# DeepNorm hybrid layer on one core: the seven-product scheme of the FFN output projection, in two groups of eight blocks with its left sums stored in DRAM

## The chip, the cores and the metric

The kernel runs on one core of a Trainium2 chip (trn2). The metric is the device time of one execution in microseconds (us); the kernel before was timed in three runs. TensorE does the matrix products (PE in the profile; its weight loads are PEld), VectorE is DVE, ScalarE is ACT, GpSimd is POOL, and SyncE is SP, whose queue issues nearly every DMA of this kernel.

## What is computed

One encoder layer on a sequence of 1024 positions and a model width of 1024: an FFN half step, attention beside a state-space scan with an output projection, a second FFN half step and a gated embedding, each followed by a layer norm. The change touches the two FFN half steps alone:

```python
def _swiglu(x, w_in, w_out):
    gate, up = jnp.split(x @ w_in, 2, axis=-1)
    return (jax.nn.silu(gate) * up) @ w_out
...
x = _layer_norm(ALPHA * x + 0.5 * _swiglu(x, ffn1_w_in[i], ffn1_w_out[i]), ln_g[i, 0], ln_b[i, 0])
...
x = _layer_norm(ALPHA * x + 0.5 * _swiglu(x, ffn2_w_in[i], ffn2_w_out[i]), ln_g[i, 2], ln_b[i, 2])
```

The hidden width is 2816, which is 22 blocks of 128. Below, h is silu(gate) * up, kept transposed: block f holds 128 hidden units by 1024 positions.

## The kernel before

**Split operands.** Every product is of float32 precision. An operand is split into a rounded part (a copy to fp32r on ACT, L100 or L400) and a remainder (a subtraction on VectorE, L82 or L401), and `mm3` (L108 to L115) issues three matmuls for each pair of blocks: high by low, low by high, high by high. A matmul of 128x128 by 128x512 is the unit of TensorE's work here.

**Making h** (`ffn_h`, `ffn_first`, `ffn_rest`). Each block f takes seven products of 12 matmuls (a seven-product scheme over the two column halves of w_in and the two halves of the positions). The weights of f come by two DMAs of 512 KB from SP (`raw`, L92); GpSimd makes their sums (L246 to L249) and adds two of the products (L331, L332); VectorE empties PSUM (L271, L326, L330, L333, L334) and multiplies (L336, L337); SP stores block f to `hD` in DRAM (L338, one DMA of 512 KB). The split weights stand in a ring of 10 buffers (`blk`), the products in four PSUM buffers (`sm`). Meanwhile, two iterations for each step, `right_sums` loads two blocks of w_out (L293, L294), makes four sums of their halves on VectorE (L299 to L302) and stores them in `wT` (L287).

**The product h by w_out** (`ffn_strassen`, then a tail). The first 16 blocks of h go through a seven-product scheme once more, in four groups of four blocks. In a group, two blocks of h make the first column of a 2 by 2 matrix of halves and two the second, and likewise with w_out. Each of the seven products has 24 matmuls (four column chunks of 128, two blocks, three passes). Three of them (called "11", "12" and "21" after the part of the result) are added from the PSUM tiles `sm` to the accumulators `acc` (L415, four 512-wide additions on VectorE); the other four go from the PSUM tiles `big`, of which there are two, to sums called M1, M5, M6 and M7: in the first group by ACT (L419), then by VectorE (L421, two 1024-wide additions). A product's left operand is a half of h as it is or a sum of halves; the sums are made here by GpSimd (`combine`, L451), which also makes some of the remainders (L401). The operands live in eight tiles named xh00 to xl11 (`pair`), two to a product, so operands for four products can be there at once. After the last group the M are added to each other (`add_sums`, L427) and to the accumulators (`add`, L432). The other six blocks of h go through the tail: two blocks in 16 units of 6 matmuls (first tail; `ffn_out`, L364 empties PSUM), then four blocks, with the layer norm.

**What sets the order.** TensorE's order is that of the code (`in_order`). The other engines' queues are laid out by a scheduler when the program is built; each engine then works through its queue in order. `issue_after` (`behind`) holds a DMA behind the SP instruction traced last. SP has one queue, so a DMA that waits for its source holds up all behind it.

Of the kernel before, what the change touches and what calls it, by code (L numbers as in the profile page):

```python
# [25 lines left out]
GRP = 2  # L26
# [10 lines left out]
class Layer:  # L37
# [236 lines left out]
    def right_sums(self, c, i, wo, groups):  # L274
# [5 lines left out]
        to = self.dram.tile([groups, 4, P, 2, 512], F32, name=f"wT{i}")  # L280
# [9 lines left out]
        def load(q):  # L290
            g, j = divmod(q, 2)
            w1, w2 = (pool.tile([P, D], F32, name=n) for n in ("wr1", "wr2"))
            nc.sync.dma_start(out=w1, in_=wo[4 * g + j])  # L293
            nc.sync.dma_start(out=w2, in_=wo[4 * g + 2 + j])  # L294
            return w1, w2, pool.tile([P, 2, 512], F32, name="wt12")

        def sums(q, w1, w2, t):
            g, j = divmod(q, 2)
# [9 lines left out]
        def step(n):  # L308
            q = n // 2
            if n % 2:  # L310
                return sums(q, *tiles[q])
            with self.behind(mybir.EngineType.SP):
                store()
                if q < 2 * groups:
                    tiles[q] = load(q)

        return pool, to, [lambda n=n: step(n) for n in range(4 * groups + 1)]

    def ffn_rest(self, X, tmp, to, blocks, p1, sg, between=None):
# [18 lines left out]
        nc.sync.dma_start(out=to, in_=sg)  # L338

    def ffn_h(self, X, wi, tmp, hD, pre=(), done=0, aside=None):  # L340
# [8 lines left out]
        for f in range(done, NF + 1):  # L349
            s = first(f) if f < NF else None  # L350
            self.pop(2)
            if prev:
                self.ffn_rest(X, tmp, hD[f - 1], self.mixed_blocks(*prev[0]), *prev[1:])
# [12 lines left out]

# [11 lines left out]
    def ffn_strassen(self, c, hD, wo, wT, acc, groups, tp, during):  # L380
# [3 lines left out]
        V, G, A = nc.vector, nc.gpsimd, nc.scalar  # L384
# [6 lines left out]
        C = {"11": (0, lo), "12": (0, hi), "21": (4, lo), "22": (4, hi)}  # L391

        def split(srcs, n, eng):

            b = self.pair()
            for i, src in enumerate(srcs):
                o = slice(0, n) if len(srcs) < n or n == 1 else slice(i, i + 1)
                if len(src.shape) == 2:
                    src = src.unsqueeze(1)
                A.copy(out=b[:, o, 0], in_=src)  # L400
                eng.tensor_tensor(out=b[:, o, 1], in0=src, in1=b[:, o, 0].bitcast(F32), op=ALU.subtract)  # L401
            return b

        def product(S, T, n, to, first=False):

            for jp in range(2):
                ps = None if to in C else self.psb()
                for q in range(2):
                    o = self.pss() if to in C else ps[:, q * 512:(q + 1) * 512]
                    c = slice((jp * 2 + q) * P, (jp * 2 + q + 1) * P)  # L410
                    self.mm3(o, [((S[:, b, 0, c], S[:, b, 1, c]), (T[:, b, 0], T[:, b, 1])) for b in range(n)])
# [22 lines left out]
        def right(g, k):  # L434
            t = tp.tile([P, 2, 512], F32, name="wT", bufs=3)
            nc.sync.dma_start(out=t, in_=wT[g, k])
            return t

        for gi, fs in enumerate(groups):
            n = len(fs) // 2  # L440
            first = fs is groups[0]
            h1 = [self.ring_raw(hD[f]) for f in fs[:n]]
            w1 = self.ring.tile([P, 2, 512], F32, name="blk")
            for i, f in enumerate(fs[:n]):
                nc.sync.dma_start(out=w1[:, i], in_=wo[f][:, lo])
            h2, w2 = [self.ring_raw(hD[f]) for f in fs[n:]], [self.ring_raw(wo[f]) for f in fs[n:]]
            s1, s2 = (tp.tile([P, 2, 512], F32, name=k)[:, :n] for k in ("s1", "s2"))

            def combine(out, a, b, op=ALU.subtract, eng=G):
                for i in range(n):  # L450
                    eng.tensor_tensor(out=out[:, i], in0=a(i), in1=b(i), op=op)  # L451

            a11, a21 = (lambda i: h1[i][:, lo]), (lambda i: h1[i][:, hi])
            a12, a22 = (lambda i: h2[i][:, lo]), (lambda i: h2[i][:, hi])
            b21, b22 = (lambda i: w2[i][:, lo]), (lambda i: w2[i][:, hi])

            def raw(x, eng=V):
                return split([x(i) for i in range(n)], n, eng)

            E = V if first else G  # L460
            last = fs is groups[-1]
            t2, t4, t1 = right(gi, 1), right(gi, 3), right(gi, 0)
            product(raw(a11), split([w1], n, V), n, 1, first)
            combine(s1, a21, a22, ALU.add)
            combine(s2, lambda i: s1[:, i], a11)
            product(raw(a12), raw(b21), n, "11")
            product(split([s2], n, V), split([t2], n, V), n, 6, first)
            t3 = right(gi, 2)
            combine(s2, a12, lambda i: s2[:, i])
            product(raw(a22, E), split([t4], n, V), n, "21")  # L470
            product(split([s1], n, V), split([t1], n, V), n, 5, first)
            combine(s1, a11, a21)
            product(split([s2], n, V), raw(b22, G), n, "12")
            if last:
                add_sums(6, 1)
                add_sums(5, 6)
            product(split([s1], n, V), split([t3], n, V), n, 7, first)
# [4 lines left out]
    def ffn_y(self, c, i, x, hD, wo, wT, weights, groups, after=None):  # L482
# [6 lines left out]
        for t in range(NT):  # L489
# [1213 lines left out]
```

## Time and profile before

| | |
|---|---|
| median of 3 runs | 2087.12 us (2084.81 to 2087.18) |
| the profiled execution, its own time | 2087.78 us |
| its span, first to last instruction | 2085.9 us |
| mean granted TensorE clock | 0.991 |
| h of FFN 1 made, until | about 476 us |
| seven-product stage of FFN 1 | 476.0 to 632.2 us |
| its first tail | 632.2 to 660.4 us |
| seven-product stage of FFN 2 | 1752.0 to 1908.7 us |
| its first tail | 1908.7 to 1936.9 us |

A row of the view by stretches gives, for a stretch of the span, its length, each engine's busy time with its number of instructions in brackets, TensorE's granted clock, the DMA engines' share and their rate. In the list of waits a row names who waited, the line and engine that ended the wait, the total, the number of waits and the longest. A matmul's shown duration (0.39 us) overlaps the next one's, so the pace of TensorE is read from how many stand in a stretch.

### The profile page before, as it was taken

The numbers are of one execution on the slowest core, as the hardware profiler recorded it, in microseconds if no ns is written. First come the engines' busy times: TensorE is split into PE (matmuls) and PEld (weight loads), VectorE is DVE, ScalarE is ACT, GpSimd is POOL, SyncE is SP. The second block draws the span as 40 slices with busy tenths as digits, with TensorE's granted clock in tenths as the row PEclk, the third lists the DMA queues.
The fourth block names the chain that finished last, engine by engine and source line by source line (L and its number), as shares of the span: only waits on it lengthen the run. The fifth ranks groups of instructions, "written<-read, shape, count | busy, mean of one in ns | idle before, by whom it ended". The sixth has DMA issues, their size and how long they took to land.

```text
span 2085.9 us, 25640 instructions
## 1 busy us (share of the span) xinstructions
PE 2014.4 (97%) x9312; PEld 1643.4 (79%) x9316; DVE 1561.8 (75%) x2353; ACT 874.8 (42%) x1610; POOL 619.7 (30%) x440
## 2 busy tenths in 40 slices
PE   7899999999999999998999999899999999999998
PEld 6688888888787888787887777778888888877886
DVE  6865565658899838648997769886666666989987
ACT  5433333336441214528888864333333334533121
POOL 0544444426530213000001001264444444541111
PEclk9999999999999999999999999999999999999999
DMA  7323433447531311230003381133334329542222
GB/s 256 118 101 122 160 123 121 151 153 282 190 122 58 119 42 36 76 96 33 1 1 104 105 302 72 71 111 141 121 121 162 121 91 341 194 141 81 71 81 81
DMA packets 94822, 254.33 MB, mean 122 GB/s; under 512 B 11586, under 2 KB 24258, under 8 KB 94696
## 3 DMA queue, kind: packets, MB, share of 16 engines
q1 hardware_dynamic: 92392, 248.51, 33.8%
q10 hardware_dynamic: 2304, 4.20, 0.5%
q8 instruction: 73, 1.20, 0.2%
q14 instruction: 53, 0.43, 0.1%
HBM read 184.84 MB, written 67.83 MB: 121 GB/s over the span
## 4 chain that ended last, share of the span: by engine, by line
PE 79%; DVE 11%; ACT 4%; DMA 3%; issue 2%; POOL 1%; SPq 0%; DVEq 0%; ACTq 0%; POOLq 0%
PE sm L114 59%; PE big L114 9%; PE big L1024 3%; PE sm L1046 3%; DVE blk L82 2%; PE sm L1061 1%; PE sm L1062 1%; DVE M L427 1%; DVE acc L415 1%; POOL qr L753 1%; DVE M L421 1%; DVE xl L82 1%; PE big L202 1%; DMA sg<-in_wi_dram 1%; ACT y L1124 1%
## 5 line engine op out<-in xcount | busy, mean ns | idle before, releaser
L114 PE MATMUL sm<-xh,blk 128*128 128x512 f32 x1440 | 452.7, 395 | 0.0
L114 PEld LDWEIGHTS sm<-xh,blk 128*128 128x128 f32 x1440 | 271.6, 189 | 64.3
L114 PE MATMUL sm<-xl,blk 128*128 128x512 f32 x720 | 285.6, 397 | 2.6 <-DVE xl L82 2.6
L114 PE MATMUL sm<-blk,xh 128*128 128x512 f32 (+2 forms) x912 | 279.1, 383 | 5.1 <-DVE blk L82 4.7
L114 PE MATMUL sm<-xl,xh 128*128 128x512 f32 x960 | 232.7, 393 | 8.0 <-DVE acc L364 7.2
L100 ACT CAST blk<-raw 128x512 fp32r<-128x512 f32 (+1 forms) x168 | 100.6, 611 | 327.9 <-PE sm L114 181.9
L114 PEld LDWEIGHTS sm<-xl,xh 128*128 128x128 f32 x960 | 178.4, 188 | 51.3 <-DVE acc L364 14.9
L114 PEld LDWEIGHTS sm<-blk,xh 128*128 128x128 f32 x912 | 169.3, 191 | 39.2 <-DVE blk L82 6.5
L82 DVE TENSOR_TENSOR blk<-s,blk 128x512 fp32r<-128x512 f32 x176 | 147.4, 841 | 69.0 <-ACT blk L100 67.2
L82 DVE TENSOR_TENSOR blk<-raw,blk 128x512 fp32r<-128x512 f32 (+1 forms) x168 | 148.6, 895 | 57.6 <-ACT blk L100 56.9
L114 PE MATMUL big<-xl,xh 128*128 128x512 f32 x768 | 180.5, 392 | 6.3 <-DVE M L421 5.2
L100 ACT CAST blk<-s 128x512 fp32r<-128x512 f32 x176 | 108.4, 622 | 161.1 <-PE sm L114 148.5
L114 PEld LDWEIGHTS big<-xl,xh 128*128 128x128 f32 x768 | 145.0, 189 | 37.7 <-ACT xl L400 6.0
L114 PE MATMUL sm<-blk,xl 128*128 128x512 f32 (+2 forms) x456 | 172.8, 379 | 0.0
L114 PEld LDWEIGHTS sm<-xl,blk 128*128 128x128 f32 x720 | 135.8, 189 | 36.2 <-DVE xl L82 4.2
L246 POOL TENSOR_TENSOR s<-raw 128x512 f32<-128x512 f32 x42 | 56.2, 1338 | 289.5 <-DVE blk L82 204.6
L177 POOL TENSOR_TENSOR ln_k<-ln_k,mhalf 128x1 f32<-128x1 f32 x32 | 40.5, 1264 | 317.3 <-DVE ln_k L176 296.7
L114 PE MATMUL sm<-xET3h,blk 128*128 128x512 f32 x352 | 110.7, 395 | 0.2 <-DVE blk L82 0.2
L114 PE MATMUL sm<-xET2h,blk 128*128 128x512 f32 x352 | 110.5, 395 | 0.1
L114 PEld LDWEIGHTS sm<-blk,xl 128*128 128x128 f32 x456 | 87.0, 191 | 15.3
L249 POOL TENSOR_TENSOR s<-raw,s 128x512 f32<-128x512 f32 x42 | 58.9, 1402 | 132.3 <-DVE blk L82 132.1
L331 POOL TENSOR_TENSOR u<-u,p 128x512 f32<-128x512 f32 x44 | 73.8, 1677 | 79.8 <-DVE u L330 79.8
(310 smaller groups left out, 4063.5 us busy)
## 6 DMA issues: line engine op xcount, KB each, us to landing
raw<-in_wi_dram SPq DMA_DIRECT2D x84, 512.0 KB
hD<-sg SPq DMA_DIRECT2D x44, 512.0 KB
blk<-hD SPq DMA_DIRECT2D x44, 512.0 KB
wr<-in_wo_dram SPq DMA_DIRECT2D x32, 512.0 KB
wT<-wT SPq DMA_DIRECT2D x32, 512.0 KB
blk<-in_wo_dram SPq DMA_DIRECT2D x28, 512.0 KB
wT<-wt SPq DMA_DIRECT2D x32, 256.0 KB
wT<-wr SPq DMA_DIRECT2D x32, 256.0 KB
```

The costliest lines, as they stand in the source:

```text
L82: (eng or self.nc.vector).tensor_tensor(out=out, in0=full, in1=hi.bitcast(F32), op=ALU.subtract)
L100: self.nc.scalar.copy(out=b[:, 0, :n], in_=src)
L114: self.nc.tensor.matmul(ps, lhsT=a, rhs=b, start=(i == 0), stop=(i == n - 1))
L177: nc.gpsimd.tensor_tensor(out=r, in0=v, in1=self.mhalf[:, :1], op=ALU.pow)
L202: nc.tensor.transpose(out=ps[:, k], in_=a[:, k * P:(k + 1) * P], identity=self.ident)
L246: G.tensor_tensor(out=s1, in0=a21, in1=a22, op=ALU.add)
L249: G.tensor_tensor(out=s4, in0=a12, in1=s2, op=ALU.subtract)
L331: G.tensor_tensor(out=u2, in0=u2, in1=p5, op=ALU.add)
L415: V.scalar_tensor_tensor(out=a, in0=o, scalar=scale, in1=a, op0=ALU.mult, op1=ALU.add)
L421: V.scalar_tensor_tensor(out=m, in0=ps, scalar=scale, in1=m, op0=ALU.mult, op1=ALU.add)
L1024: nc.tensor.matmul(ps[:, n * 512:(n + 1) * 512], lhsT=Q[:, h, q0:q0 + P], rhs=K[:, h // 4, j, n * 512:(n + 1) * 512], start=j == 0, stop=j ...
L1046: nc.tensor.transpose(out=pt[:, k], in_=pr[:, kk * P:(kk + 1) * P], identity=self.ident)
```

## The change

**Groups.** The 16 blocks go in two groups of eight instead of four groups of four. The even blocks of a group are the first column of the 2 by 2 matrix, the odd ones the second, so the sums of h take neighbouring blocks. A product has 48 matmuls, and its operands take four of the eight tiles xh00 to xl11. The number of matmuls and the sizes of the tiles are as before; each sum M and each accumulator is added to half as often.

**Left factors.** `left_factors` makes the sums of h in `ffn_h`, on VectorE, as soon as a block is there: one for an even block, three for an odd one (tiles h1, h2, h3). All seven left factors of a group go to `hS` in DRAM: two DMAs of 256 KB for an even block and five for an odd one, where one DMA of 512 KB stood before. Blocks 16 to 21 go to `hD` as before. The pool of h tiles (`sg`) has three buffers in both FFNs (before: two in the first, three in the second).

**Streaming.** Each product loads its own operands (`operand`): two DMAs of 512 KB for the left, two of 512 KB or four of 256 KB for the right, into ring tiles; then ACT copies and VectorE subtracts, four times each, 1024 wide. GpSimd has no work in this stage. The accumulators' initial values are loaded in quarters (`load`), each just ahead of the product that adds to it first, where they were all loaded ahead of the stage.

The diff, cut to its core:

```diff
-    def right_sums(self, c, i, wo, groups):
+    def right_sums(self, c, i, wo):
...
-            nc.sync.dma_start(out=w1, in_=wo[4 * g + j])
-            nc.sync.dma_start(out=w2, in_=wo[4 * g + 2 + j])
+            nc.sync.dma_start(out=w1, in_=wo[2 * q])
+            nc.sync.dma_start(out=w2, in_=wo[2 * q + 1])
...
+    def left_factors(self, i, tmp):
...
+        def store(f, h):
+            if f >= NS:
+                nc.sync.dma_start(out=hD[f - NS], in_=h)
+                return
+            g, j = divmod(f // 2, GRP // 2)
+
+            def put(k, src):
+                nc.sync.dma_start(out=hS[g, k, :, j], in_=src)
+
+            def combine(name, a, b, op=ALU.subtract):
+                t = tmp.tile([P, 512], F32, name=name)
+                V.tensor_tensor(out=t, in0=a, in1=b, op=op)
+                return t
+
+            if f % 2 == 0:
+                put(0, h[:, lo])
+                put(6, combine("h3", h[:, lo], h[:, hi]))
+                even.append(h)
+            else:
+                e = even.pop()
+                put(1, h[:, lo])
+                put(3, h[:, hi])
+                s1 = combine("h1", e[:, hi], h[:, hi], ALU.add)
+                s2 = combine("h2", s1, e[:, lo])
+                put(4, s1)
+                put(2, s2)
+                put(5, combine("h3", h[:, lo], s2))
...
-        nc.sync.dma_start(out=to, in_=sg)
+        to(sg)
...
+        def operand(src):
+
+            blocks = []
+            for u in range(n // 2):
+                r = self.ring.tile([P, 2, 512], F32, name="blk")
+                src(u, r)
+                b = self.pair()
+                A.copy(out=b[:, :, 0], in_=r)
+                V.tensor_tensor(out=b[:, :, 1], in0=r, in1=b[:, :, 0].bitcast(F32), op=ALU.subtract)
+                blocks += [b[:, i] for i in range(2)]
+            return blocks
...
+            L, R = operand(left), operand(right)
...
-                    self.mm3(o, [((S[:, b, 0, c], S[:, b, 1, c]), (T[:, b, 0], T[:, b, 1])) for b in range(n)])
+                    self.mm3(o, [((l[:, 0, c], l[:, 1, c]), (r[:, 0], r[:, 1])) for l, r in zip(L, R)])
...
-            combine(s1, a21, a22, ALU.add)
-            combine(s2, lambda i: s1[:, i], a11)
-            product(raw(a12), raw(b21), n, "11")
-            product(split([s2], n, V), split([t2], n, V), n, 6, first)
...
+        for g in range(NS // GRP):
+            first, last = g == 0, g == NS // GRP - 1
+            f = g * GRP
+            for k, right, to in ((0, plain(f, lo), 1), (1, plain(f + 1, lo), "11"), (2, summed(wT[g, 1]), 6), (3, summed(wT[g, 3]), "21"),
+                                 (4, summed(wT[g, 0]), 5), (5, plain(f + 1, hi), "12"), (6, summed(wT[g, 2]), 7)):
+                if first and to in C:
+                    with self.behind(mybir.EngineType.SP):
+                        load(*C[to])
+                if last and k == 6:
+                    add_sums(6, 1)
+                    add_sums(5, 6)
+                product(summed(hS[g, k]), right, to, first)
...
-        out = c.enter_context(tc.tile_pool(name=f"fo{i}", bufs=n))
+        out = c.enter_context(tc.tile_pool(name=f"fo{i}", bufs=3))
```

**The order at three places.** First, the place where one group gives way to the next, in FFN 1. Before, VectorE's queue from the end of the second group's "12" to the start of the third group (M70 and M71 are the two halves of M7, the group's last product, M10 and M11 those of M1, the next group's first; `big` are the PSUM tiles they come from; xh00 to xl01 are operands of later products):

```order
L415 SCALAR_TENSOR_TENSOR acc0_2_3653<-sm_4234,acc0_2_3653 128x512
L415 SCALAR_TENSOR_TENSOR acc0_3_3654<-sm_4242,acc0_3_3654 128x512
L401 TENSOR_TENSOR xh00_4397<-s2_4308,xh00_4397 128x2x512
L401 TENSOR_TENSOR xl00_4400<-wT_4309,xl00_4400 128x2x512
L421 SCALAR_TENSOR_TENSOR M70_3673<-big_4264,M70_3673 128x1024
L421 SCALAR_TENSOR_TENSOR M71_3674<-big_4278,M71_3674 128x1024
L401 TENSOR_TENSOR xl01_4448<-wT_4311,xl01_4448 128x2x512
L421 SCALAR_TENSOR_TENSOR M10_3683<-big_4323,M10_3683 128x1024
```

Now there is one such place in a stage, behind the first group, where M7 is taken from PSUM by ACT. ACT's queue there (L469 is what L419 was, L439 the copy of a split; xh10 to xl11 are operands of the second group's first product, xh00 to xl01 of the one after it):

```order
L439 CAST xl10_4344<-blk_4342 128x2x512
L439 CAST xl11_4356<-blk_4353 128x2x512
L469 ACTIVATE M70_3774<-big_4273 128x1024
L439 CAST xh00_4413<-blk_4411 128x2x512
L439 CAST xh01_4424<-blk_4421 128x2x512
L469 ACTIVATE M71_3775<-big_4299 128x1024
L439 CAST xl00_4418<-blk_4416 128x2x512
L439 CAST xl01_4430<-blk_4427 128x2x512
```

and VectorE's, up to the second addition to M1 (L440 is the subtraction of a split, L471 the addition to a sum M; the L83 rows split a weight of the stage that follows):

```order
L440 TENSOR_TENSOR xl11_4356<-blk_4353,xl11_4356 128x2x512
L440 TENSOR_TENSOR xh00_4413<-blk_4411,xh00_4413 128x2x512
L440 TENSOR_TENSOR xh01_4424<-blk_4421,xh01_4424 128x2x512
L440 TENSOR_TENSOR xl00_4418<-blk_4416,xl00_4418 128x2x512
L440 TENSOR_TENSOR xl01_4430<-blk_4427,xl01_4430 128x2x512
L471 SCALAR_TENSOR_TENSOR M10_3784<-big_4359,M10_3784 128x1024
L83 TENSOR_TENSOR blk_4647<-blk_4645,blk_4647 128x512
L83 TENSOR_TENSOR blk_4650<-blk_4645,blk_4650 128x512
L440 TENSOR_TENSOR xh10_4499<-blk_4497,xh10_4499 128x2x512
L471 SCALAR_TENSOR_TENSOR M11_3785<-big_4385,M11_3785 128x1024
```

Before, M7 of this place stood on VectorE behind two splits; now its first half stands on ACT behind splits that an earlier product's end releases, and on VectorE there are four splits, each 1024 wide, between one product's results and the next.

Second, VectorE's queue at the end of this stage. Before, from the additions to M7, which the stage's last product makes (L364 empties the first tail's units):

```order
L421 SCALAR_TENSOR_TENSOR M70_3673<-big_4870,M70_3673 128x1024
L421 SCALAR_TENSOR_TENSOR M71_3674<-big_4884,M71_3674 128x1024
L82 TENSOR_TENSOR xh11_5099<-blk_5100,xh11_5099 128x512 x2
L364 SCALAR_TENSOR_TENSOR acc0_0_3651<-sm_4930,acc0_0_3651 128x512
L82 TENSOR_TENSOR xl11_5106<-blk_5107,xl11_5106 128x512 x2
L364 SCALAR_TENSOR_TENSOR acc0_0_3651<-sm_4938,acc0_0_3651 128x512
```

and in the changed kernel (L405 is what L364 was, L477 what L427 was):

```order
L471 SCALAR_TENSOR_TENSOR M70_3774<-big_4835,M70_3774 128x1024
L83 TENSOR_TENSOR blk_5112<-blk_5110,blk_5112 128x512
L83 TENSOR_TENSOR blk_5115<-blk_5110,blk_5115 128x512
L477 TENSOR_TENSOR M60_3789<-M60_3789,M70_3774 128x1024
L83 TENSOR_TENSOR blk_5120<-blk_5118,blk_5120 128x512
L477 TENSOR_TENSOR M70_3774<-M70_3774,M50_3779 128x1024
L83 TENSOR_TENSOR xh10_5074<-blk_5075,xh10_5074 128x512 x2
L471 SCALAR_TENSOR_TENSOR M71_3775<-big_4861,M71_3775 128x1024
L83 TENSOR_TENSOR xh11_5088<-blk_5089,xh11_5088 128x512 x2
L405 SCALAR_TENSOR_TENSOR acc0_0_3760<-sm_4919,acc0_0_3760 128x512
L83 TENSOR_TENSOR xl10_5081<-blk_5082,xl10_5081 128x512 x2
```

Two additions of M to M and three splits for the second tail now stand between the two halves of M7; before, the halves stood together and those came later.

Third, SP's queue while h of FFN 1 is made, one pair of blocks before:

```order
L92 DMA raw<-in_wi_dram 128x1024 x2
L338 DMA hD_87<-sg 128x1024
L287 DMA wT_103<-wt_1020 128x512 x2
L287 DMA wT_103<-wr_1016 128x512
L287 DMA wT_103<-wr_1017 128x512
L293 DMA wr_1313<-in_wo_dram 128x1024
L294 DMA wr_1314<-in_wo_dram 128x1024
```

and now:

```order
L93 DMA raw<-in_wi_dram 128x1024 x2
L338 DMA hS_102<-sg 128x512 x2
L338 DMA hS_102<-h_1343 128x512
L338 DMA hS_102<-h_1345 128x512
L338 DMA hS_102<-h_1349 128x512
L292 DMA wT_107<-wt_1050 128x512 x2
L292 DMA wT_107<-wr_1046 128x512
L292 DMA wT_107<-wr_1047 128x512
L93 DMA raw<-in_wi_dram 128x1024
L297 DMA wr_1356<-in_wo_dram 128x1024
L298 DMA wr_1357<-in_wo_dram 128x1024
L93 DMA raw<-in_wi_dram 128x1024
```

Each store of an h sum waits for VectorE, and the weight loads of a later block stand behind three such stores in every other block.

126 lines of the change are left out of this document (53 added, 73 removed).

## The prediction

> **What bounds the kernel now.** I read the page's busy times, then the stretches of the FFN stages, then who waited for whom in them. The page's first part and the slices of PE:
>
> ```profile
> PE 2014.4 (97%) x9312; PEld 1643.4 (79%) x9316; DVE 1561.8 (75%) x2353; ACT 874.8 (42%) x1610; POOL 619.7 (30%) x440
> PE   7899999999999999998999999899999999999998
> ```
>
> TensorE is the bound nearly everywhere, so a change that leaves the matmuls as they are (this one does: 14 products of 48 for 28 of 24) can only take away TensorE's idle time, or add to it. The stretches: the first row lies in the making of h, then come stage and first tail of FFN 1 and of FFN 2.
>
> ```profile
> core 0: us, PE busy (x) PEld busy (x) DVE busy (x) ACT busy (x) POOL busy (x), PEclk, DMA share, GB/s
> 400.00:450.00 50.00, 50.00 (x216) 40.23 (x215) 30.74 (x41) 16.68 (x26) 18.18 (x14) 1.00 0.25 98
> 476.00:632.20 156.20, 152.64 (x672) 125.80 (x671) 142.98 (x153) 75.61 (x102) 75.96 (x46) 1.00 0.54 189
> 632.20:660.40 28.20, 24.19 (x98) 17.39 (x96) 28.20 (x42) 4.47 (x8) 0.00 (x0) 1.00 0.06 19
> 1752.00:1908.70 156.70, 153.99 (x673) 127.08 (x672) 142.95 (x154) 73.98 (x100) 76.11 (x45) 0.99 0.54 186
> 1908.70:1936.90 28.20, 24.19 (x97) 17.40 (x97) 28.20 (x42) 4.46 (x8) 0.00 (x0) 1.00 0.14 46
> ```
>
> The pace to hold these against is in the chain of waits: 24 matmuls with nothing between them.
>
> ```profile
> 561.65 5.44 PE sm L114 x24
> 567.09 5.44 PE big L114 x24
> ```
>
> A stage of 672 matmuls takes 28 x 5.44 = 152.3 us at that pace; it took 156.2 and 156.7, so 3.9 and 4.4 us are idle. The first tail's 96 matmuls take 4 x 5.44 = 21.8 us; they took 28.2 twice, so 6.4 us each are idle. All that the change can win here is 3.9 + 4.4 + 6.4 + 6.4 = 21.1 us. TensorE's waits name the cause, in FFN 1 (first three rows) and FFN 2:
>
> ```profile
> PE sm L114 <- DVE acc L364: 3.7, 5, 1.3
> PE big L114 <- DVE M L421: 2.5, 1, 2.5
> PE big L114 <- DVE xl L401: 1.1, 1, 1.1
> PE sm L114 <- DVE acc L364: 3.5, 4, 1.3
> PE big L114 <- DVE M L421: 2.7, 1, 2.7
> ```
>
> Every one is a wait for VectorE, which is 143 of 156 us busy in the stages and without a gap in the first tails. The wait of 2.5 us, in VectorE's own timeline:
>
> ```profile
> 550.55 1.87 DVE L415 SCALAR_TENSOR_TENSOR acc<-sm,acc 128x512 f32<-128x512 f32 x3
> 552.34 1.21 DVE L401 TENSOR_TENSOR xh<-s,xh 128x1024 fp32r<-128x1024 f32 x1
> 553.47 1.21 DVE L401 TENSOR_TENSOR xl<-wT,xl 128x1024 fp32r<-128x1024 f32 x1
> 554.61 2.34 DVE L421 SCALAR_TENSOR_TENSOR M<-big,M 128x1024 f32<-128x1024 f32 x2
> ```
>
> M7's first half, which frees a PSUM tile, stands behind a backlog, and M1 of the next group follows M7 at once and needs that tile.
>
> **Part 1: the stage.** VectorE's rows in FFN 1's stage before:
>
> ```profile
> L401 DVE TENSOR_TENSOR xl<-wT,xl 128x1024 fp32r<-128x1024 f32 x16 | 27.3, 1710 | 0.9 <-ACT xl L400 0.9
> L421 DVE SCALAR_TENSOR_TENSOR M<-big,M 128x1024 f32<-128x1024 f32 x22 | 26.5, 1217 | 9.3 <-PE big L114 9.3
> L400 ACT CAST xl<-wT 128x1024 fp32r<-128x1024 f32 x16 | 16.6, 1047 | 0.2 <-DMA wT<-wT 0.2
> L451 POOL TENSOR_TENSOR s<-blk,s 128x512 f32<-128x512 f32 x8 | 13.9, 1765 | 33.1 <-DVE xh L401 33.1
> L427 DVE TENSOR_TENSOR M<-M,M 128x1024 f32<-128x1024 f32 x4 | 5.5, 1377 | 0.0
> L401 DVE TENSOR_TENSOR xl<-blk,xl 128x1024 fp32r<-128x1024 f32 x3 | 3.6, 1213 | 0.0
> L82 DVE TENSOR_TENSOR xl<-blk,xl 128x512 fp32r<-128x512 f32 x4 | 2.6, 679 | 0.0
> ```
>
> The same 1024-wide subtraction takes 1.71 us in one row and 1.21 in another; beside it GpSimd reads SBUF in the stage. [...] I take 1.21, and 1.71 as the upper end.
>
> VectorE's work in a stage is then 56 splits x 1.21 = 67.8; 24 additions to `acc` x 0.68 = 16.3; 8 to M (the second group alone) x 1.22 = 9.8; 8 weight and 12 tail splits x 0.68 = 13.6; 6 sums of M x 1.21 = 7.3: 115 us of 152.3, for 143 now (143 again with splits at 1.71). ACT has 56 x 1.05 plus little; both fit.
>
> What matters is the latest chain. Four operand tiles to a product leave two products in flight: when product k ends, the splits for k+2 must be done while k+1 runs, in 48 x 5.44/24 = 10.88 us. The fullest place in the order is the last product of the second group: the first copy 1.05, four splits 4.84, one M addition 1.22, one sum of M 1.21 and one `acc` addition 0.68 = 9.0 us. That leaves 1.9 us. The M7-to-M1 meeting occurs once, and M7's first half is there taken by ACT: half a product, 5.4 us, ahead of need. So I cost the stage's idle at zero, a gain of 3.9 and 4.4 us; without that cover the same 2.5 us wait comes back. At the stage's start the loads of the first products stand in SP's queue ahead of all but one quarter of the accumulators, and VectorE's order has the first splits before the last block of h is out of PSUM; the 1.1 us wait for `xl` has nothing that would keep it.
>
> **Part 2: the first tail.** Its 16 units of 6 matmuls, 1.36 us each, go through four PSUM tiles, so unit n waits for eviction n-4.
>
> ```profile
> 637.95 0.68 DVE L364 SCALAR_TENSOR_TENSOR acc<-sm,acc 128x512 f32<-128x512 f32 x1
> 638.55 1.27 DVE L82 TENSOR_TENSOR xl<-blk,xl 128x512 fp32r<-128x512 f32 x2
> ```
>
> VectorE steps at 0.60 us for 512 and (2.34 - 1.21, above) 1.13 for 1024. By the new order, the last stage product's 10.88 us hold a first copy of 0.7 (estimate), 13 instructions of 512 and 3 of 1024, 11.9 us: VectorE is 1.0 late at the tail's start. Up to the seventh eviction stand 22 more of 512 and 3 of 1024: 1.0 + 13.2 + 3.4 = 17.6 us. The eleventh unit starts then, and six units take 8.2: the tail ends after 25.8 us, not 28.2. Gain 2.4 us each time, 4.8 in all. Bounds: 0 to 6.4 each.
>
> **Part 3: making h.** Added on VectorE: four sums for two blocks, two SBUF inputs each. Rows of FFN 1 (the waits of SP from 150 to 450 us, the others from 100):
>
> ```profile
> L82 DVE TENSOR_TENSOR blk<-raw,blk 128x512 fp32r<-128x512 f32 x52 | 48.8, 941 | 23.6 <-ACT blk L100 23.2
> L301 DVE TENSOR_TENSOR wr<-wr,wr 128x512 f32<-128x512 f32 x8 | 9.9, 1237 | 0.0
> L302 DVE TENSOR_TENSOR wr<-wr,wt 128x512 f32<-128x512 f32 x8 | 5.4, 681 | 0.0
> ACT blk L100 <- PE sm L114: 147.7, 72, 2.2
> DVE sg L271 <- DMA hD<-sg: 31.8, 18, 3.1
> SPq L338 <- DVE sg L337: 148.9, 16, 17.9
> ```
>
> At 0.68 to 1.24 each they are 2.7 to 5.0 us in 168/216 x 50 = 38.9 us (two blocks), on an engine that is 31 of 50 us busy. Three stand together behind an odd block, ahead of L271, which empties PSUM for the next block: 2.0 to 3.7 us later. Four PSUM tiles of 2.8 us each cover 8.4, and the wait of L271 for the store of h (31.8 us in 18 blocks) should go with the third buffer. ACT's copies wait for TensorE to free ring buffers, so the operands are as far ahead as ten buffers allow. Cost: zero; if the cover were gone, up to 3.7 us for each of 16 odd blocks.
>
> The DMAs: SP issues 17 for two blocks, not 12, and the weight loads stand behind three stores that wait for those sums. SP waits for h 149 us of the 300 between 150 and 450 us. A weight load and its use, in SP's and ACT's timelines of FFN 2:
>
> ```profile
> 1606.43 1.31 SPq L287 DMA_DIRECT2D wT<-wr  x2
> 1611.44 4.93 SPq L92 DMA_DIRECT2D raw<-in_wi_dram  x2
> 1635.07 0.62 ACT L100 CAST blk<-raw 128x512 fp32r<-128x512 f32 x1 [1.69 <-issue]
> ```
>
> Issued by 1616.4, copied at 1635.1: 18.7 us. Five issues at 0.66 and three sums make it up to 7.0 us later. Cost zero.
>
> **Sum.** 3.9 + 4.4 + 4.8 = 13.1 us. The profiled execution's own time, 2087.8 us, is its span of 2085.9 and 1.9 around; it stands 0.7 above the median of 2087.1, so I forecast 2087.1 - 13.1 = 2074 us.
>
> **The rivals.**
>
> *All idle goes.* VectorE has 28 us less in a stage; if the order's late start in the tail is made up, all 21.1 us go: 2066 us. Against it: the order puts M7's sums ahead of the tail's evictions.
>
> *The waits return elsewhere.* Lookahead is two products; VectorE takes over GpSimd's splits. If one operand is 0.5 us late in each of 24 products, 12 us are lost and the gain with it: 2083 to 2091 us, no change. It decides where the chain of 9.0 us passes 10.9, that is, with splits above 1.68 us. For it: the row at 1.71. Against: GpSimd is idle there.
>
> *Slower: the stream is too thin.* Each product now loads 2 MiB, 2.10 MB in 10.88 us = 193 GB/s, and the accumulators 4.2 MB more over the first five or six products, some 260 GB/s. The busiest stretch now:
>
> ```profile
> 486.00:498.00 12.00, 10.92 (x48) 8.74 (x47) 11.17 (x11) 7.61 (x10) 10.64 (x6) 1.00 1.03 411
> ```
>
> 411 GB/s came in pieces of 512 and 256 KB, the sizes used now. It would decide below 193 GB/s: at 170 a product takes 12.4 us, 1.5 more, 14 x 2 x 1.5 = 42 us, against 13 gained: 2116 us. For it: queue order, since SP waits for ring buffers in turn. [...]
>
> *The change doesn't do what it says* is ruled out by the order: no GpSimd instruction is left in the stage.
>
> **Chances.** Forecast 0.62, its own range 2069 to 2080; all idle gone 0.12; no change 0.12; slower 0.14. Range 2065 to 2091: it leaves out the slower case and little else. About 0.2%, 4.2 us, is what a measurement of this kernel can tell from no change: faster 0.74, same 0.12, slower 0.14.
>
> **What would show it.** Right: both stages at 152 to 153 us with 672 matmuls, no wait of `big` for VectorE, first tails near 26 us, splits at 1.21 us, h still at 216 matmuls in 50 us. Wrong: idle time before each product with an operand as its releaser; a DMA as the releaser of ACT's copies there; or fewer than 216 in 50 us in the making of h.

## The result

The changed kernel takes 2069.24 us, the median of 4 runs (2067.39 to 2070.09), against 2087.15 for the kernel before, 4 runs beside it (2084.81 to 2087.80): a ratio of 0.9915, 95% interval 0.9898 to 0.9932, or 17.9 us less. The forecast was 2074, its range 2065 to 2091, faster at 0.74. A second set of 5 runs gave 2068.13, ratio 0.9918 (0.9904 to 0.9931).

The page of the changed kernel, busy times (the span is 2068.2 us, 2085.9 before):

```profile
PE 2007.2 (97%) x9316; PEld 1641.1 (79%) x9316; DVE 1536.6 (74%) x2325; ACT 867.6 (42%) x1570; POOL 479.0 (23%) x348
```

The shares hardly moved. The stretches tell more; the rows stand for the same places as those of before: making of h, stage and first tail of FFN 1, stage and first tail of FFN 2, and the busiest 12 us of the stream.

```profile
core 0: us, PE busy (x) PEld busy (x) DVE busy (x) ACT busy (x) POOL busy (x), PEclk, DMA share, GB/s
400.00:450.00 50.00, 50.00 (x217) 40.55 (x216) 31.43 (x41) 16.67 (x26) 19.17 (x14) 1.00 0.27 96
476.20:628.50 152.30, 152.30 (x673) 126.12 (x672) 102.99 (x112) 69.67 (x83) 1.35 (x2) 1.00 0.69 239
628.50:654.10 25.60, 22.96 (x98) 17.71 (x96) 25.60 (x41) 4.88 (x9) 0.00 (x0) 1.00 0.14 44
1741.10:1893.50 152.40, 152.40 (x674) 126.17 (x673) 103.18 (x112) 69.59 (x83) 0.00 (x0) 1.00 0.68 237
1893.50:1919.30 25.80, 23.02 (x98) 17.74 (x97) 25.80 (x41) 4.86 (x9) 0.00 (x0) 1.00 0.21 63
486.00:498.00 12.00, 12.00 (x55) 9.93 (x54) 6.70 (x8) 5.88 (x7) 0.00 (x0) 1.00 1.03 405
```

Both stages take 152.3 to 152.4 us, and PE's busy time equals the stretch: no idle time is left there. VectorE works 103 us in a stage, not 143, GpSimd 1 us, not 76. The first tails take 25.6 and 25.8 us, not 28.2. In the chain of waits every product is now one unbroken piece of 48 matmuls:

```profile
563.39 10.88 PE sm L115 x48
574.27 10.88 PE big L115 x48
```

TensorE's waits from the stage's start to the end of the first tail, FFN 1 and then FFN 2, are one row each:

```profile
PE sm L115 <- DVE acc L405: 2.6, 4, 1.3
PE sm L115 <- DVE acc L405: 2.8, 4, 1.3
```

The waits for `M` (2.5 and 2.7 us) and for `xl` (1.1) are gone; what is left lies in the first tail. VectorE's two costliest groups in FFN 1's stage, shapes apart:

```profile
L440 DVE TENSOR_TENSOR xh<-blk,xh 128x1024 fp32r<-128x1024 f32 x25 | 30.2, 1220 | 28.7 <-ACT xh L439 28.7
L440 DVE TENSOR_TENSOR xl<-blk,xl 128x1024 fp32r<-128x1024 f32 x25 | 29.7, 1217 | 0.4 <-ACT xl L439 0.4
```

Every split takes 1.22 us. VectorE now sits idle 28.7 us of the stage until ACT has made a copy: its backlog has become slack.

The terms of the sum, predicted and measured: stage FFN 1 -3.9 and -3.9 (156.2 to 152.3), stage FFN 2 -4.4 and -4.3 (156.7 to 152.4), first tails -2.4 each and -2.6, -2.4. Together 13.1 predicted, 13.2 measured. The medians differ by 17.9, so 4.7 us came from elsewhere. By the stretches 4.6 of them lie between the end of FFN 1's first tail and the start of FFN 2's stage (1091.6 us before, 1087.0 now). Most of what runs there the change doesn't touch; the making of h of FFN 2, which it does touch, lies there too.

### The profile page after: what moved, and what is told of

It is laid out like the page before. It is cut to its first block, busy times and chain, and to the rows that moved or that the text cites. A ratio compares the mean times of both kernels' runs of the same rounds, so it can differ in the third digit from the quotient of the medians.

```text
span 2068.2 us, 25696 instructions
## 1 busy us (share of the span) xinstructions
PE 2007.2 (97%) x9316; PEld 1641.1 (79%) x9316; DVE 1536.6 (74%) x2325; ACT 867.6 (42%) x1570; POOL 479.0 (23%) x348
## 4 chain that ended last, share of the span: by engine, by line
PE 86%; DVE 6%; ACT 3%; issue 3%; DMA 2%; POOL 0%; SPq 0%; DVEq 0%; ACTq 0%; POOLq 0%
PE sm L115 64%; PE big L115 11%; PE big L1048 3%; PE sm L1070 3%; PE sm L1085 1%; PE sm L1086 1%; DVE blk L83 1%; PE big L203 1%; DVE xl L83 1%; DMA sg<-in_wi_dram 1%; PE sm L1165 0%; DVE acc L405 0%; PE sm L1154 0%; DMA blk<-hD 0%; DMA raw<-in_xT_dram 0%
## 5 line engine op out<-in xcount | busy, mean ns | idle before, releaser
L83 DVE TENSOR_TENSOR blk<-s,blk 128x512 fp32r<-128x512 f32 x176 | 149.6, 854 | 71.4 <-ACT blk L101 68.8
L83 DVE TENSOR_TENSOR blk<-raw,blk 128x512 fp32r<-128x512 f32 (+1 forms) x168 | 153.9, 924 | 45.7 <-ACT blk L101 44.9
L247 POOL TENSOR_TENSOR s<-raw 128x512 f32<-128x512 f32 x42 | 62.6, 1491 | 331.6 <-DVE blk L83 223.6
L440 DVE TENSOR_TENSOR xh<-blk,xh 128x1024 fp32r<-128x1024 f32 x56 | 67.7, 1220 | 65.4 <-ACT xh L439 65.4
L115 PE MATMUL sm<-xl,xh 128*128 128x512 f32 x384 | 95.9, 395 | 5.4 <-DVE acc L405 5.4
L115 PE MATMUL big<-xh,xh 128*128 128x512 f32 x384 | 97.5, 389 | 0.0
L115 PE MATMUL big<-xl,xl 128*128 128x512 f32 x384 | 97.5, 389 | 0.0
L439 ACT CAST xh<-blk 128x1024 fp32r<-128x1024 f32 x56 | 56.3, 1047 | 91.1 <-PE big L115 38.6
```

The source lines that it names most:

```text
L83: (eng or self.nc.vector).tensor_tensor(out=out, in0=full, in1=hi.bitcast(F32), op=ALU.subtract)
L115: self.nc.tensor.matmul(ps, lhsT=a, rhs=b, start=(i == 0), stop=(i == n - 1))
L247: G.tensor_tensor(out=s1, in0=a21, in1=a22, op=ALU.add)
L439: A.copy(out=b[:, :, 0], in_=r)
L440: V.tensor_tensor(out=b[:, :, 1], in0=r, in1=b[:, :, 0].bitcast(F32), op=ALU.subtract)
```

## The experiments

**The same two kernels again.** No edit; second profiles, for those 4.7 us.

> The changed kernel once more, for a second profile. Expected of both theories: 2069 us, stages of 152.3 us, first tails of 25.6 to 25.8 us. About 4.3 of the 17.9 us gained came from stages that the change does not touch, where the stretches of about 3.4 us at a granted clock of 0.5 numbered 10 before and 6 after, at some 1.5 us each. Theory 'fixed': these stretches stand at the same places in every execution of the same program, so the profile shows the same six, at 66, 933, 940, 1309, 1360 and 2063 us, each within 1 us. Rival 'chance': they fall differently in each execution, so at least two of the six are elsewhere or gone.

> The kernel before once more, for a second profile. Theory 'fixed': the same ten stretches at a granted clock of 0.5 (66, 844, 943, 950, 1138, 1203, 1247, 1322, 1831 and 2080 us), span 2086 within 1 us. Rival 'chance': another number of them, between 5 and 12, and a span that differs by about 1.5 us for each stretch more or fewer. If this profile has about six, the 4.3 us outside the changed stages are no part of what the change brought.

Measured: the changed kernel 2068.13 us (span 2064.8), the kernel before 2081.72 (span 2079.9), 6.0 us less than the span of its first profile. Over all runs beside the experiments the kernel before lay between 2077.9 and 2092.6. Its two profiles at one place of an unchanged stage, first and second execution: the same matmul waits 1.35 us for the same operand. First execution:

```profile
1133.53 0.50 PE L114 MATMUL sm<-blk,xh 128*128 128x512 f32 x1 [0.56 <-DVE blk L82]
1135.83 0.50 PE L114 MATMUL sm<-blk,xh 128*128 128x512 f32 x1 [1.35 <-DVE blk L82]
1137.04 0.50 PE L114 MATMUL sm<-blk,xh 128*128 128x512 f32 x1 [0.24 <-DVE blk L82]
```

and second:

```profile
1131.35 0.50 PE L114 MATMUL sm<-blk,xh 128*128 128x512 f32 x1 [0.57 <-DVE blk L82]
1133.65 0.50 PE L114 MATMUL sm<-blk,xh 128*128 128x512 f32 x1 [1.35 <-DVE blk L82]
1134.85 0.50 PE L114 MATMUL sm<-blk,xh 128*128 128x512 f32 x1 [0.24 <-DVE blk L82]
```

What follows those gaps, as stretches of 3.4 us (the column before the last two is the granted clock), in the first execution:

```profile
1137.80:1141.20 3.40, 3.40 (x9) 2.65 (x8) 2.82 (x4) 3.40 (x16) 0.00 (x0) 0.50 0.20 74
```

and in the second:

```profile
1134.90:1138.30 3.40, 3.40 (x15) 2.70 (x15) 3.30 (x5) 3.40 (x16) 0.00 (x0) 1.00 0.46 184
```

2.15 us of gaps within some 4 us were followed by 3.4 us at half clock in one execution, with 9 matmuls, and by full clock in the other, with 15. So 'fixed' falls; 'chance' holds, but chance over fixed places: in the first profiles the nine stretches of the kernel before and the five of the changed one ahead of the last matmul all stand behind gaps, some 1.5 to 2.6 us of idle time in the 3.4 us ahead of each, and at the place above the second execution has the same gaps. What decides between the two outcomes of one gap is not shown.

How much was run so, over the whole span, is estimated from the mean granted clocks, taking the clock to be 1.00 or 0.50 as in the two rows above: 0.991 over 2085.9 us and, in the second profile, 0.992 over 2079.9 us before; 0.994 over 2068.2 us and 0.995 over 2064.8 us after.

At half clock a share of 2 x (1 - clock) was run: 37.5 and 33.3 us before, 24.8 and 20.6 after, 12.7 us less in the mean. Half of that, 6.4 us, is the most that it costs by this estimate, with a matmul half as fast at 0.50 (the rows have 9 for 15); up to 0.9 of it is already in the sum, as one stretch of 3.4 us stands in FFN 2's stage, behind the wait of 2.7 us, in one of the two profiles of before. The rest, up to 5.5 us, has the size of the 4.7 us that the stages leave unexplained. The clocks of the other runs go further: over 58 runs of the kernel before, on three chips, the mean is 0.9920, over the 9 of the changed kernel 0.9938, so by the same estimate 16.7 and 12.9 us are lost to half clock, 3.9 less. Fewer stretches are then no accident of the four profiles; why the changed kernel has fewer is open. The mean times of these runs, 2084.4 and 2068.5, are 15.9 us apart, so about 2 us of the 17.9 are the luck of the first few runs.

**Groups of four.** The same sums and stream, the group size of before:

```diff
-GRP = 8
+GRP = 4
```

> The changed kernel with four groups of four blocks in place of two groups of eight (the same sums; products half as long, still streamed, still no GpSimd in the stage). VectorE per stage: 56 splits x 1.21 = 67.8, 48 additions to acc x 0.68 = 32.6, 24 to M x 1.22 = 29.3, 20 small splits x 0.68 = 13.6, 6 sums of M 7.3: 150.6 of 152.3 us, for 115 now. Theory 'VectorE's load': TensorE waits again for M and acc, 2 to 6 us in each stage, 2073 to 2081 us. Rival 'the stream and the idle GpSimd are what helped': stages stay at 152 to 153 us, 2069 us.

Measured: 2095.14 us, ratio to before 1.0042 (1.0026 to 1.0058). Its stage and first tail of FFN 1, then stage and first tail of FFN 2:

```profile
477.90:630.30 152.40, 152.40 (x674) 126.15 (x673) 132.08 (x149) 71.33 (x83) 0.89 (x1) 1.00 0.70 242
1753.60:1919.10 165.50, 154.53 (x674) 127.50 (x673) 132.86 (x149) 71.32 (x83) 0.00 (x0) 0.97 0.64 215
630.30:658.40 28.10, 24.10 (x97) 17.36 (x96) 28.10 (x42) 4.40 (x8) 0.00 (x0) 1.00 0.12 38
1919.10:1947.70 28.60, 24.20 (x98) 17.42 (x97) 28.60 (x43) 4.37 (x8) 0.00 (x0) 1.00 0.19 65
```

Neither theory held whole. VectorE is 132 us busy, not the 150.6 that I worked out from durations (instructions overlap; their steps are 0.60 and 1.13 us), and at 132 of 152 us no product of FFN 1's stage waits. So that stage's gain does not need groups of eight. The first tails do: at 28.1 and 28.6 us they are those of the kernel before. And FFN 2's stage has one wait of 11.0 us, in front of its third product (the expectation of the next run calls it the second), with ACT's row at its end:

```profile
1766.59 1.14 ACT L101 CAST blk<-blk 128x512 fp32r<-128x512 f32 x2
1774.50 1.94 ACT L469 ACTIVATE M<-big 128x1024 f32<-128x1024 f32 x2 [6.78 <-DMA hD<-sg]
```

The first copy into `M` waits for the store of the last block of h, whose memory `M` reuses. This stage and the two tails are 18.4 us longer than in the changed kernel, of the 26 to 27 in all. The mean clock of the six runs, 0.987, has, by the estimate above, 14 us more lost to half clock than the changed kernel has, 5 of them in this stage (0.97 of 165.5 us), which is about the rest.

**That store through another queue.**

```diff
-                nc.sync.dma_start(out=hD[f - NS], in_=h)
+                nc.gpsimd.dma_start(out=hD[f - NS], in_=h)
```

> The groups of four again, with the last six blocks of h stored to DRAM through GpSimd's DMA queue in place of SP's. In the groups of four TensorE waited once for 11.0 us, in FFN 2's second product, for ACT's first copy into M, and that copy for the store of the last block of h, which SP issued at 1767.3, behind the loads of the first products, and whose memory M reuses. Theory 'the store's place in SP's queue': that wait goes, stage FFN 2 falls from 165.5 to 152.4 to 155 us and the time from 2095 to 2080 to 2084 us. Rival 'the loads themselves are late, the store is only the last of what the copy waits for': the stage stays at 160 us or more. Of both: VectorE stays at 132 of 152 us in the stage and no product waits for it.

Measured: 2090.06 us, 1.0031 (1.0019 to 1.0044); the stage took 161.9 us. The wait shrank, and did not go:

```profile
PE big L115 <- ACT M L469: 7.1, 1, 7.1
```

In ACT's timeline the copy into `M` now stands right behind a weight's copy that waited for its own load:

```profile
1760.73 1.14 ACT L101 CAST blk<-blk 128x512 fp32r<-128x512 f32 x2 [2.96 <-DMA blk<-in_wg_dram]
1761.78 1.93 ACT L469 ACTIVATE M<-big 128x1024 f32<-128x1024 f32 x2
```

The rival's side: the store was the last of several late things (11.0 us became 7.1), and behind it came a load at the crowded start of the stage (404 GB/s from 1755 to 1776 us in the groups of four without this edit). In groups of eight the same copy runs no earlier, and it too waits for a DMA:

```profile
1758.24 1.94 ACT L469 ACTIVATE M<-big 128x1024 f32<-128x1024 f32 x2 [3.40 <-DMA blk<-wT]
```

That is 17.1 us after the stage's start at 1741.1, as late as in the run above (17.2; 1761.8, with a start at 1744.6). But TensorE needs the PSUM tile for the third product only, which starts 21.8 us after the stage does, and not 10.9. So in FFN 2 the longer products are what covers this wait, with 2.7 us to spare.

**The kernel before with nothing on GpSimd.**

```diff
-def combine(out, a, b, op=ALU.subtract, eng=G):
+def combine(out, a, b, op=ALU.subtract, eng=V):
...
-E = V if first else G
+E = V
...
-product(split([s2], n, V), raw(b22, G), n, "12")
+product(split([s2], n, V), raw(b22, V), n, "12")
```

> The kernel before with nothing but GpSimd's 46 instructions of the stage moved to VectorE (groups, sums and loads as before). VectorE steps at 0.60 us for 512 elements and 1.13 for 1024: 135 of the one and 63 of the other, 152 us in a stage of 152.3 without waits. Theory 'load': VectorE is full, each wait that stood there stays and others join, stages of 156 to 166 us, 2087 to 2107 us. Rival 'contention alone was the cost': stages fall to 152 to 153 us as in the changed kernel, 2076 to 2079 us.

Measured: 2085.01 us, 0.9999 (0.9989 to 1.0009): no difference. The stages:

```profile
476.00:632.50 156.50, 154.18 (x673) 127.22 (x672) 150.94 (x196) 75.40 (x102) 0.00 (x0) 0.99 0.53 189
1752.10:1908.80 156.70, 154.20 (x673) 127.19 (x672) 150.37 (x195) 74.02 (x100) 0.00 (x0) 0.99 0.53 185
```

VectorE is 151 us busy, no longer 143, and the stages are as long as before. One wait is left in each, FFN 1 and FFN 2:

```profile
PE big L114 <- ACT xl L400: 2.3, 1, 2.3
PE big L114 <- DVE M L421: 2.5, 1, 2.5
```

Both stand where M7 gives way to M1; in the first, ACT's copy and VectorE's addition to M7 end within 0.1 us of each other. The 1.1 us wait for `xl` in FFN 1 is gone, and a granted clock of 0.99 over 156.5 us, some 1.6 us by the estimate from the mean clock, makes up for it in this execution. So 'load' holds in time, at its lower end, and not in every wait: to idle GpSimd is worth nothing when VectorE takes its work.

**The changed kernel with a quarter of the splits on GpSimd.**

```diff
+def operand(src, last=V):
...
-V.tensor_tensor(out=b[:, :, 1], in0=r, in1=b[:, :, 0].bitcast(F32), op=ALU.subtract)
+(last if u else V).tensor_tensor(out=b[:, :, 1], in0=r, in1=b[:, :, 0].bitcast(F32), op=ALU.subtract)
...
-L, R = operand(left), operand(right)
+L, R = operand(left), operand(right, nc.gpsimd)
```

> The changed kernel with one split in four of the stage (the second half of each right operand) on GpSimd: 14 instructions of 1024 elements a stage, about 3.5 us each, 49 us of GpSimd, and VectorE's other 42 splits beside it at up to 1.71 us, 72 us for 68. Theory 'the idle GpSimd is not what helped, since VectorE has room to wait': stages of 152 to 153 us, 2068 to 2070 us. Rival 'contention': a split of 3.5 us on GpSimd and slower ones beside it pass the 10.88 us of a product, 1 us or more for each of 14 products a stage, 2096 us or more.

Measured: 2069.20 us, 0.9932 (0.9914 to 0.9951), as without the edit; stages 152.3 and 152.4 us. The line's instructions in FFN 1's stage (durations as minimum, median, maximum in ns):

```profile
L440 POOL TENSOR_TENSOR xl<-blk,xl x13: 2416/2872/3468, 474.5 to 606.1; 128x1024 fp32r<-128x1024 f32 x13
L440 DVE TENSOR_TENSOR xl<-blk,xl x12: 1216/1221/3432, 487.2 to 606.7; 128x1024 fp32r<-128x1024 f32 x12
```

Beside GpSimd's splits, of 2.4 to 3.5 us, VectorE's take 1.22 us in the median and up to 3.4, and nothing waits for it in the stage; the tails, where VectorE has no slack, grow to 26.5 and 27.1 us. With the run above: the gain of the stage is not an idle GpSimd. What remains is VectorE's work taken out (143 us to 103, and 132 is still enough in FFN 1), together with left sums that come ready by DMA; no run has one of the two without the other.

**Every load twice.**

```diff
+        dp = c.enter_context(self.tc.tile_pool(name="dp", bufs=2))
...
                 src(u, r)
+                src(u, dp.tile([P, 2, 512], F32, name="dummy"))
```

> The changed kernel with every operand load of the stage issued twice, the second into a tile that nothing reads: 4 MiB for a product in 10.88 us, 386 GB/s instead of 193, and twice the loads in SP's queue. Theory 'the stream has room': 411 GB/s stood over 12 us before, so the stages stay within 2 us of 152.3, 2068 to 2073 us. Rival 'the stream is near its end': at 300 GB/s a product takes 14 us, 3.1 us more on 28 products, 2155 us.

Measured: 2104.10 us, 1.0092 (1.0077 to 1.0108), between the two theories. Sixty us of FFN 1's stage, and then the whole stages:

```profile
500.00:560.00 60.00, 60.00 (x266) 49.73 (x265) 33.44 (x33) 28.72 (x32) 0.00 (x0) 1.00 0.98 365
...
476.80:639.50 162.70, 155.32 (x674) 128.00 (x672) 103.85 (x112) 69.52 (x83) 0.00 (x0) 0.97 0.95 350
1763.70:1921.30 157.60, 154.06 (x673) 127.11 (x672) 104.45 (x113) 70.95 (x84) 0.00 (x0) 0.99 0.95 351
```

At 365 GB/s, DMA busy to 98%, TensorE missed nothing for 60 us; each stage then has one long wait (7.4 and 3.5 us), and the second tails one each (5.8 and 4.6), at a time when loads still queue; whether late loads are what they hang on wasn't followed. By DMA's busy share of 95% in the stages, 350 GB/s is near the end of this stream (an estimate from that share), and the changed kernel needs 239. The rival 'too thin' of the prediction, which decided below 193 GB/s, had no ground, as the row of 411 GB/s had said. The 365 GB/s here came in pieces of 512 and 256 KB from SP's queue.

**The sums of h, twice and not at all.** Twice:

```diff
                 V.tensor_tensor(out=t, in0=a, in1=b, op=op)
+                V.tensor_tensor(out=t, in0=a, in1=b, op=op)
```

> The changed kernel with each of the four sums of two blocks of h made twice on VectorE (the second overwrites the first with the same values): 32 instructions more in the making of each h, 64 in all, 0.60 to 0.68 us each, 38 to 44 us of VectorE. Theory 'covered': VectorE is about 60% busy there and four PSUM tiles and ten ring buffers stand ahead of it, so 2068 us within 2, and 216 matmuls still take 50 us. Rival 'the sums are on the path': up to 44 us more, 2112 us. [...]

and left out:

```diff
-put(6, combine("h3", h[:, lo], h[:, hi]))
+put(6, h[:, hi])
...
-put(4, s1)
-put(2, s2)
-put(5, combine("h3", h[:, lo], s2))
+put(4, e[:, hi])
+put(2, e[:, lo])
+put(5, h[:, lo])
```

> The changed kernel without the four sums of two blocks of h: the halves of h are stored in their places (the same seven stores and bytes for two blocks), so the left factors of three products are not the sums, and the output is not the layer's. It takes 32 instructions of VectorE out of each making of h. Theory 'covered' (the prediction's part 3 at zero): TensorE has no wait in the making of h with the sums in, so without them 2068 us within 2, and 216 matmuls in 50 us still. Rival 'the sums are partly paid': the doubled sums cost 7.8 us, and if the cost is even from the first sum on, the time falls by as much, to 2060 us.

Measured: 2075.90 us doubled (0.9962, 0.9949 to 0.9976), 2067.94 without (0.9920, 0.9905 to 0.9934), beside 2068.13 and 2069.24 as they are. The single sums are covered; 32 more in each FFN are not. Their waits, making of h of FFN 1 and of FFN 2 with doubled sums:

```profile
PE sm L115 <- DVE sg L272: 2.8, 4, 1.6
PE sm L115 <- DVE sg L272: 3.4, 1, 3.4
```

Each is the wait that the prediction named: L272, which empties PSUM for the next block, stands behind the sums. In VectorE's timeline of the longest one:

```profile
1371.35 1.63 DVE L342 TENSOR_TENSOR h<-sg,h 128x512 f32<-128x512 f32 x1
1372.91 0.68 DVE L272 TENSOR_TENSOR sg<-p,sm 128x512 f32<-128x512 f32 x1
```

**The first tail's order.** Three edits of VectorE's order in the tail. In the first the splits for the second tail stand behind evictions, the additions of `M` to `acc` behind the sixth tile or later, the sums of M6 and M7 last:

```diff
+        def rest():
+            add_sums(6, 7)
+            add_sums(7, 5)
+            for j in range(4):
+                add("21", 6, j)
+                add("22", 7, j)
...
+                with self.behind(mybir.EngineType.DVE):
+                    if 1 <= t <= 4:
+                        later += tail([(f + 1 + t, in_x if t < 3 else in_ring)])
+                    for a in adds[max(t - 5, 0) * 3:max(t - 4, 0) * 3]:
+                        a()
```

> The changed kernel with VectorE's order in the first tail turned round: evictions of acc first, the splits for the second tail spread over units 3 to 10, the additions of M1 and M5 to acc behind unit 10, the sums of M6 and M7 and their additions behind the last eviction (beside the second tail). Same sums. Theory 'order': the 3.8 us above 21.8 that are left in each first tail are waits for VectorE's order alone; first tails fall from 25.7 to 22 to 23.5 us, the second tails take up to 1 us more, 2062 to 2067 us. Rival 'load': VectorE has the same work in tails one and two, so the waits come back in the second tail: 2069 us within 2.

Measured: 2094.97 us, 1.0047 (1.0033 to 1.0060). The tail did what was expected, 23.3 us both times,

```profile
625.50:648.80 23.30, 22.25 (x97) 17.76 (x96) 20.93 (x34) 5.42 (x11) 0.00 (x0) 1.00 0.14 46
```

and TensorE then waited for the first norm of the second tail, 11.0 us in each FFN:

```profile
PE big L203 <- POOL ln_k L178: 22.0, 2, 11.0
```

In the second, the first two tiles' norms are ahead of `rest()`:

```diff
+                for t in range(2):
+                    self.ln_apply(*stats[t], lnp)
+                with self.behind(mybir.EngineType.DVE):
+                    adds[8]()
```

> The order of the first tail turned round as before, but with the norms of the first two tiles ahead of the sums of M6 and M7 and their eight additions, which now stand behind the second tail's third tile. The earlier order brought the first tail to 23.3 us and then let TensorE wait 11 us twice for the first norm, behind those sums. Theory 'only the order of norm and sums was wrong': first tails 23.3 us as there, the 11 us waits fall below 3 us each, 2062 to 2068 us. Rival 'VectorE's load': all the work is still there before TensorE can turn the third tile, so the wait comes back one or two tiles later, 5 us or more each time, and the time is 2070 to 2085 us.

Measured: 2091.80 us, 1.0041 (1.0024 to 1.0058); tails of 23.9 us, and the wait came back at the third tile:

```profile
PE big L203 <- DVE ln_k L179: 21.2, 2, 11.2
```

In the third, only the additions are late, and the sums stay where they were:

```diff
+                    if 1 <= t <= 4 and f + 2 < NF:
+                        later += tail([(f + 1 + t, in_x if t < 3 else in_ring)])
+                    for a in adds[max(t - 3, 0) * 2:max(t - 2, 0) * 2] if t < 7 else adds[8:]:
+                        a()
```

> The first tail once more: sums of M6 and M7 as early as the changed kernel has them, evictions of acc ahead of the splits for the second tail (units 3 to 10), additions of M1 and M5 behind units 9 to 14, those of M6 and M7 behind the last eviction, and the first norm ahead of the second tail's last eviction of its fourth tile. Theory 'order': first tails of 23 to 24 us for 25.7, no wait of more than 3 us for a norm, 2062 to 2067 us. Rival 'load': VectorE has no idle time from the stage's end to the norm, so what is put behind comes back as a wait for a norm, 5 us or more each time: 2070 to 2092 us.

Measured: 2072.77 us, 0.9943 (0.9931 to 0.9956): faster than before, slower than the changed kernel.

```profile
625.80:650.90 25.10, 22.55 (x98) 17.70 (x96) 24.80 (x39) 5.36 (x10) 0.00 (x0) 1.00 0.13 43
```

The tails gain 0.5 and 0.7 us (the second's row has 25.10 us as well), and TensorE waits 2.7 us in front of FFN 1's first norm; the time is some 4 us above the changed kernel's, and the rest of that is not traced. My theory 'order' fell three times: the first tail can be shortened by order, but VectorE is busy from the stage's end to the norms, and what is put off meets TensorE there. Part of it may still be order (the steps of one norm stand far apart among other work); that isn't settled. None of the three beats the changed kernel.

## Why the prediction was right

- *What bounds it.* TensorE's idle time behind VectorE's backlog: right. The waits for `M` and `xl` went, and those for `acc` shrank.
- *Part 1, the stage at zero idle.* Right in size (3.9 and 4.4; 3.9 and 4.3), in FFN 2 in part by luck: of the 4.4 us that I took for idle time only 2.7 are a wait; the 1.7 left have the size of what one stretch of 3.4 us at half clock costs (1830.8 to 1834.2 us in the first profile, clock 0.51). In the second profile of the kernel before the stage has no such stretch, and with its wait of 2.6 us it is 1.5 us shorter:

```profile
1747.50:1902.70 155.20, 152.57 (x673) 126.05 (x672) 141.71 (x153) 74.18 (x100) 74.95 (x45) 1.00 0.55 188
```

  The splits fell to 1.22 us, as taken. In the two stages of the kernel before, of the 1024-wide splits that stand alone in VectorE's timeline, the 28 that no instruction of GpSimd overlaps took 1.21 to 1.23 us, the 40 that one overlaps 1.21 to 2.31. But the two runs that move work off GpSimd and onto it show that the gain doesn't rest on this. The load was put too high: 115 us from durations, 103 measured. The chain of 9.0 us to a product was never tight; VectorE idles 28.7 us before splits. That the M7-to-M1 meeting occurs only once was part of my cover; with four groups it occurs three times and costs nothing in FFN 1, which speaks for the backlog as the cause and for the meeting as only its place. That the streaming has no part in it isn't shown.
- *Part 2, the tail at 25.8 us.* 25.6 and 25.8. Of the 6.4 us of a tail that I called idle before, the row has 4.0 idle (24.19 busy of 28.2); the rest is matmuls that came slower than 5.44 us for 24. The sum had the eleventh unit start 17.6 us into the tail; in FFN 1 it started after 17.3 (645.8). Of the waits the longest is at the seventh unit, for the third eviction, which the sum doesn't name; the one at the eleventh is the second longest:

```profile
638.66 4.37 PE L115 MATMUL sm<-xl,xh 128*128 128x512 f32 x18 [1.28 <-DVE acc L405]
...
645.80 0.50 PE L115 MATMUL sm<-xl,xh 128*128 128x512 f32 x1 [0.74 <-DVE acc L405]
```

- *Part 3, the sums at zero.* Right: without them the time is the same. The cover is thinner than I held it to be: doubled, they cost 7.8 us. The wait for the store of h (31.8 us in 18 blocks) is gone, as was expected of the third buffer; VectorE's row for that line is now a short wait for TensorE:

```profile
DVE sg L272 <- PE sm L115: 2.9, 3, 1.0
```

- *The rivals.* 'All idle goes' (2066): wrong in the tails, where 3.8 to 4.0 us over 21.8 are left. 'The waits return elsewhere' and 'the stream is too thin' did not come, and the doubled loads show how much room the second had.
- *What the sum lacked.* It treated all stages but these as fixed. 4.7 of the 17.9 us lie outside, and fewer stretches at half clock can hold most of them (by estimate up to 5.5 us from the profiles, 3.9 from the clocks of all runs), with the luck of the first runs. So the forecast was 4.8 us high, for a reason that no step named.

## What to carry to other kernels

Look for the engine with a backlog and ask which of its work can be done earlier, in a stage where it has room: 40 us less of VectorE's work in a stage of 152, with the left sums loaded ready-made, was worth its 3 to 4 us of waits, while moving GpSimd's work of the stage to VectorE was worth nothing. Where VectorE had no slack up to the next stage's first need, a new order only moved the wait (to 11.0, 11.2 and 2.7 us in three runs). And before a gain of a few us in untouched stages is explained, profile the same program twice.

## What the runs showed of the hardware

- Gaps of 2.15 us in TensorE's work were followed by 3.4 us at a granted clock of 0.50 in one execution of the kernel before (9 matmuls for 15, an estimated 1.4 to 1.7 us: six matmuls, or half the stretch), and by a clock of 1.00 in another (the two rows at 1137.8 and 1134.9).
- TensorE's pace differed between stages. 48 matmuls of the seven-product stage take 10.88 us, 226.7 ns each; in the making of h, in the chain of waits of the changed kernel, 216 take 50.19 us, 232.4 ns each:

```profile
399.91 50.19 PE sm L115 x216
```

  The groups by shape of the changed kernel, from 400 to 450 us and from 500 to 600 us, have the same difference of 6 ns in the mean of one:

```profile
L115 PE MATMUL sm<-xl,blk 128*128 128x512 f32 x44 | 17.4, 395 | 0.0
...
L115 PE MATMUL big<-xl,xl 128*128 128x512 f32 x125 | 31.9, 389 | 0.0
```

  Size, type and clock are the same; the first has an operand in a ring buffer (`blk`), the second none. Whether it is the place in SBUF that does it wasn't tried.
- The pace also differed between two executions of one program. The kernel before made h of FFN 1 at 233.3 ns a matmul in its first execution and at 232.4 in the second:

```profile
399.86 50.17 PE sm L114 x215
...
399.81 50.19 PE sm L114 x216
```

  Over 22 blocks of 84 matmuls that is some 1.8 us (an estimate), of the 6.0 us between the two spans.
